# A hybrid decoder block on one core: the warm-up and the last tile of its first norm, one small load, and the product of a bias table

## The chip, the cores and the metric

The kernel runs on one core of a Trainium2 chip. The metric is the device time of one execution in microseconds, the median of several runs. A core has five engines that run in parallel and wait for each other by semaphores: TensorE (PE, matrix products and transposes; PEld is its weight load), VectorE (DVE), ScalarE (ACT), GpSimd (POOL) and SyncE (SP). DMAs are issued from the queues of SP, ACT and POOL. TensorE writes into PSUM, eight banks of 128 partitions by 512 floats, which VectorE and ScalarE empty.

## The reference

One layer on 512 tokens of width 1024, float32. Cut to what matters here:

```python
h = rmsnorm(x, attn_norm_g)                 # first norm
proj = h @ w_in                             # one combined projection, split into columns of
                                            # queries, 3 x (keys, values), gates, RWKV inputs, 2 merge gates
o_a = nsa_mixer(...)                        # compressed + selected + window attention, T5 bias table rel_bias
o_b = rwkv7_mixer(...)                      # RWKV-7 recurrence, 8 heads of 64
merged = sigmoid(gate_a) * (o_a @ w_proj_a) + sigmoid(gate_b) * (o_b @ w_proj_b)
x = x + merged @ w_out
h2 = rmsnorm(x, ffn_norm_g)
x = x + conv_ffn(h2, ...)                   # 2 x 2816 wide, causal conv of width 3, SiLU gate
```

In `nsa_mixer`, keys and values of overlapping blocks of 32 tokens go through `gelu(flat @ w1) @ w2` (the "compression"), and every score gets `rel_bias[t5_bucket(t - s)]` added.

## The kernel before

**Products.** The products with float32 weights are made from parts: a weight tile of 512 KB is loaded by SP into one of three `raw` buffers (`wload`, L267), split into a rounded half `hi` (`whi`, mostly ScalarE) and a remainder `lo` (`wlo`, L296, VectorE or GpSimd), and each product is the sum hi x hh + hi x hl + lo x hh, where `hh` and `hl` are the same two halves of the transposed activations. A `raw` buffer is loaded again when its split is done, a `whi` or `wlo` buffer (two each) is written again when TensorE is through with it. `weight_tiles` fixes the order of all weight tiles, and so the order of SP's queue.

**Order of the work.** Most of it is put in order by a planner that works with estimated costs; within `tc.manual_schedule(...)` the engines named there keep the order of the source. The DMAs of SP keep their place among the weight loads.

**First norm** (L326 to L376, in an order written by hand for TensorE, ScalarE, VectorE and GpSimd). `ident` (128x128) is loaded on ScalarE's queue (L154); 16 transposes of it by itself (`NWARM`, L329) run before any real work. For each of the four token tiles `t`: ScalarE sums squares (into `hs[t]`) and takes the square root, VectorE makes the reciprocal root (`rstd1`) and scales the tile (`ts`, L131; the last tile in two pieces of 512 columns), TensorE transposes it in blocks of 128 columns into eight banks `pts[k]` (`turn`, L335). For tiles 0 to 2 the transposes follow at once; those of the last tile come at the end, block by block. After tile 1, two more transposes turn the loaded parameter rows `pr0` (norm gain) and `pra` (RWKV parameters, eight small loads on GpSimd's queue, L162) into columns, in `pt`. ScalarE then splits the first weight tile (`hi`), and copies the gain to `ang`; VectorE copies the parameters to `prm` and makes `omm` = 1 - mu from them; GpSimd copies one element of `omm` into `lo` (L355), which its next instruction overwrites, and then makes `lo` in two halves (L357). For each block `k` ScalarE writes `hh[:, k]` and VectorE `hl[:, k]` (L136) from the bank. The first product `p0` takes the bank of block 0.

**Bias table** (L682 to L690, planned). A one-hot matrix (33 x 384) and the table (33 x 8, with a row for masked places) are loaded into corners of `QK`; one product (8 x 384) gives the bias by distance, ScalarE copies it to `vb`, and one DMA on ScalarE's queue writes it 16 times to a table `vd` in HBM. `bias_rows` reads that much later. The area of `vb` is written again by the key copies `kn` of `kv_proj(0, 256)`, which therefore wait for the DMA.

**Compression** (`compress`). Its four steps `s4` each take two weight tiles (`cmp_w1_k`, `cmp_w1_v`) and run as fillers between the steps of the RWKV recurrence. Within step `s4 == 1` SP is given the two loads of `cmp_w2` (64 KB each, L805) into `QK`; they are read after the last step. The recurrence's values `UV` are copied from PSUM by ScalarE and VectorE at each of its steps.

Of the kernel before, what the change touches and what calls it, by code (L numbers as in the profile page):

```python
# [11 lines left out]
F32 = mybir.dt.float32  # L12
# [9 lines left out]
D = 1024  # L22
NT = S // 128
# [18 lines left out]
ROWS = {}  # L42
# [39 lines left out]
def hybrid_block(ctx: ExitStack, tc: tile.TileContext, A: dict, out: bass.AP):  # L82
    nc = tc.nc
    v, sc, te = nc.vector, nc.scalar, nc.tensor
    NWARM = 16

    def dbg(name, ap):
        if name in DBG:
# [31 lines left out]
    def mm(o, l, r, start, stop):  # L120
        te.matmul(o, lhsT=l, rhs=r, start=start, stop=stop)  # L121

    def act(o, i, f=AF.Copy, **kw):
        sc.activation(o, i, f, **kw)  # L124
# [4 lines left out]
    def ts(o, a, s1, s2, op0=ALU.mult, op1=ALU.add):  # L129
        if s2 is None:  # L130
            v.tensor_scalar(o, a, s1, None, op0=op0)  # L131
        else:
            v.tensor_scalar(o, a, s1, s2, op0=op0, op1=op1)
# [6 lines left out]
    ident, mask, ones, cmask = kc[:, 0:128], kc[:, 128:256], kc[:, 256:384], kc[:, 384:416]  # L140
# [3 lines left out]
    xp_cm, xp = pool("x")  # L144
# [2 lines left out]
    v.memset(eps1, 1e-6)  # L147
    one = xp.tile([128, 1], F32, name="one")
    v.memset(one, 1.0)
    act(one, one, AF.Sqrt)  # L150
    pr0 = xp.tile([8, 128], F32, name="pr0")
    for t in range(NT):
# [4 lines left out]
    for name in ("rwkv_mu", "rwkv_w0", "rwkv_a0", "rwkv_k_k", "rwkv_k_a", "rwkv_r_k", "rwkv_ln_g", "rwkv_ln_b"):  # L157
        r0, n = ROWS[name]
# [10 lines left out]
    def cols(name):  # L169
        r0, n = ROWS[name]  # L170
        return prm[:, r0:r0 + n]
# [154 lines left out]
    with tc.manual_schedule(engines={getattr(mybir.EngineType, e) for e in ("PE", "Activation", "DVE", "Pool")}):  # L326
        pts = [mmb() if k < 4 else pa() if k < 6 else pb() for k in range(KT)]
        for i in range(NWARM):
            te.transpose(pts[7][:, 384:512], ident, ident)  # L329
        hi = wp.tile([128, KT, 128], F32R, name="whi", tag="whi", bufs=2)  # L330
        lo = wp.tile([128, KT, 128], F32R, name="wlo", tag="wlo", bufs=2)
        raw = loads.pop(0)[0]

        def turn(t, k):
            te.transpose(pts[k][:, 128 * t:128 * t + 128], hs[t][:, 128 * k:128 * k + 128], ident)  # L335

        for t in range(NT):
            r = ssx[:, t:t + 1]
            act(hs[t], xt[:, t], AF.Square, accum_out=r)
            rstd1(r)  # L340
            for c0 in ((0, 512) if t == NT - 1 else (0,)):
                c1 = 512 + c0 if t == NT - 1 else D
                ts(hs[t][:, c0:c1], xt[:, t, c0:c1], r, None)
            if t < NT - 1:
                for k in range(KT - t // 2):
                    turn(t, k)
            if t == 1:
                pt = pts[7][:, 384:512]
                te.transpose(pt[:, 0:8], pr0, ident[0:8, 0:8])
                te.transpose(pt[:, 8:8 + NR0], pra, ident[0:NR0, 0:NR0])  # L350
        act(hi, raw)
        act(ang, pt[:, 0:8])
        v.tensor_copy(prm[:, 0:NR0], pt[:, 8:8 + NR0])
        ts(omm, cols("rwkv_mu"), -1.0, 1.0)
        nc.gpsimd.tensor_copy(lo[:, 0, 0:1], omm[:, 0:1])  # L355
        for i in (slice(0, 4), slice(4, 8)):
            nc.gpsimd.tensor_tensor(lo[:, i], raw[:, i], hi[:, i].bitcast(F32), op=ALU.subtract)  # L357
        late.append(nc.gpsimd.tensor_copy)
        wsplit()
        for k in range(KT):  # L360
            for t in range(NT - 1 - k // 7, NT):
                turn(t, k)
            act(hh[:, k], pts[k], AF.Copy, scale=ang[:, k:k + 1])
            stt(hl[:, k], pts[k], ang[:, k:k + 1], hh[:, k].bitcast(F32), ALU.mult, ALU.subtract)
        ts(w0h, cols("rwkv_w0"), 0.5, None)
        ts(kah, cols("rwkv_k_a"), 0.5, None)
        ts(a0h, cols("rwkv_a0"), 0.5, None)
        ts(oma, cols("rwkv_k_a"), -0.5, 1.0)
        p0 = mmb()
        for k in range(KT):  # L370
            mm(p0, hi[:, k], hh[:, k], k == 0, False)
            if k:
                mm(p0, lo[:, k - 1], hh[:, k - 1], False, False)
            mm(p0, hi[:, k], hl[:, k], False, False)
        mm(p0, lo[:, KT - 1], hh[:, KT - 1], False, True)
# [237 lines left out]
    for k in range(31):  # L613
        m, n = 31 - k, k + 1
# [64 lines left out]
    windows(1, dense_fm(hh, hl))  # L679


    oh, rbx, vb = QK[0:33, 2048:2432], QK[0:33, 2440:2448], QK[0:8, 2560:2944]  # L682
    nc.gpsimd.memset(rbx[32:33], NEG)
    sc.dma_start(rbx[0:32], A["rel_bias"])
    sc.dma_start(oh, A["onehot"])
    pt = pa()
    mm(pt[0:8, 0:384], rbx, oh, True, True)
    act(vb, pt[0:8, 0:384])
    vd = dp.tile([8, 16 * 385], F32, name="vd")
    sc.dma_start(vd.rearrange("h (i m) -> h i m", m=385)[:, :, 0:384], vb[:, None, :].to_broadcast([8, 16, 384]))  # L690

    def kv_proj(b, n):
        bkv = yield from dense_tok_g(n, hh, hl)
# [85 lines left out]
    def compress():  # L779
        Rk = [sg1[:, 2 * a:2 * a + 2].rearrange("p m s -> p (m s)").rearrange("p (j g n) -> p j g n", j=16, g=2)  # L780
              for a in range(2)]
        for a, s_ in enumerate("kv"):
            v.memset(Rk[a][:, :, :, 31:32], 0.0)
            r0 = ROWS["cmp_pe_" + s_][0]
            for g in range(2):
                dv = Dc[:, a, g].rearrange("p (n j) -> p j n", j=8)
                for jh in range(2):
                    tt(Rk[a][:, 8 * jh:8 * jh + 8, g, 0:31], dv[:, :, jh:31 + jh],
                       prm[:, r0 + 8 * jh:r0 + 8 * jh + 8, None].to_broadcast([128, 8, 31]), ALU.add)
        cw2, hid, hidT, kcd = (QK[:, o:o + 256] for o in range(3072, 4096, 256))  # L790
        cw2 = cw2.rearrange("p (a m d) -> p a m d", a=2, m=2)
        hidT = hidT.rearrange("p (m a n) -> p m a n", m=2, a=2)
        kcd = kcd[0:32].rearrange("p (g a d) -> p g a d", g=2, a=2)
        kcs = cp.tile([32, 2], F32, name="kcs")
        yield
        hx = mmb()[:, 0:256]
        for s4 in range(4):
            w = [wnext(4, 256) for _ in range(2)]
            for j in range(4):
                for a in range(2):  # L800
                    mm(hx[64 * a:64 * a + 64], Rk[a][:, 4 * s4 + j].rearrange("p g n -> p (g n)"), w[a][:, j],
                       s4 + j == 0, s4 + j == 6)
            if s4 == 1:
                for a, s_ in enumerate("kv"):
                    nc.sync.dma_start(cw2[:, a], A["cmp_w2_" + s_][0].rearrange("(m p) d -> p m d", p=128))  # L805
            yield
        act(hid, hx, AF.Square)
        ts(hid, hid, 0.044715, 1.0)
        tt(hid, hid, hx, ALU.mult)
        act(hid, hid, AF.Tanh, scale=math.sqrt(2.0 / math.pi))  # L810
        stt(hid, hid, 1.0, hx, ALU.add, ALU.mult)
        yield
        pt = mmb()
        for m in range(2):
            te.transpose(pt[:, 128 * m:128 * m + 128], hid[:, 128 * m:128 * m + 128], ident)
        act(hidT.rearrange("p m a n -> p (m a n)"), pt[:, 0:256])
        yield
        kc_ps = mmb()
        for g in range(2):
            for m in range(2):  # L820
                mm(kc_ps[0:32, 64 * g:64 * g + 64], hidT[:, m, 0, 32 * g:32 * g + 32], cw2[:, 0, m], m == 0, m == 1)
        nc.gpsimd.memset(vcb, 0.0)
        for g in range(2):
            for e in range(2):
                bs = slice(64 * g + 32 * e, 64 * g + 32 * e + 32)
                for m in range(2):
                    mm(kc_ps[bs, 128:192], hidT[:, m, 1, 32 * g:32 * g + 32], cw2[:, 1, m], m == 0, m == 1)
        for g in range(2):
            for e in range(2):
                bs = slice(64 * g + 32 * e, 64 * g + 32 * e + 32)  # L830
                act(vcb[bs, 2 * g + e], kc_ps[bs, 128:192], AF.Copy, scale=0.5)
        for g in range(2):
            act(kcd[:, g, 0], kc_ps[0:32, 64 * g:64 * g + 64], AF.Copy, scale=0.5)
            act(kcd[:, g, 1], kcd[:, g, 0], AF.Square, accum_out=kcs[:, g:g + 1])
        rstd(kcs, DH)
        for g in range(2):
            ts(kcd[:, g, 1], kcd[:, g, 0], kcs[:, g:g + 1], None)
            ts(kcd[:, g, 0], kcd[:, g, 0], kcs[:, g:g + 1], None)
        yield
        pt = mmb()  # L840
        for g in range(2):
# [534 lines left out]
```

## Time and profile before

| | |
|---|---|
| median of 3 runs | 837.51 us (837.49 to 838.12) |
| profiled execution, its time | 838.0 us |
| its span in the profile | 836.2 us |
| TensorE busy | 822.0 us (98%) |
| VectorE busy | 515.8 us (62%) |
| ScalarE busy | 407.2 us (49%) |
| GpSimd busy | 51.5 us (6%) |

The profile is of one execution. Its span runs from the first to the last instruction; the device time holds some 1.8 us more around it. Busy time of an engine is the union of its instructions. A timeline row gives start, duration, engine, line, operation, written tile <- read tiles, shapes, the number of instructions merged into it, and in brackets the idle time before it and what ended that. Rows that end in q (SPq, ACTq) are DMA issues. Starts of consecutive products tell TensorE's pace; their durations overlap. The list of waits gives, for engine and line, what was waited for: microseconds in total, how many times, the longest.

### The profile page before, as it was taken

The page shows a single profiled execution, that of the slowest core. Times are in us where ns is not written, and L with a number is a line of the kernel's source. Part 1 is how long each engine was busy: PE and PEld are TensorE (multiplying, and loading weights), DVE is VectorE, ACT ScalarE, POOL GpSimd, SP SyncE. Part 2 cuts the span into 40 slices and gives each one's busy share as a digit, 9 for nine tenths or more (in the row PEclk, how much of TensorE's full clock was granted, in tenths as well). Part 3 has the DMA queues.
Part 4 walks back from the last instruction along what each step waited for, and adds up shares of the span by engine and source line. Part 5 has one row for each costly group of instructions (what it writes and reads, how often), then busy time and mean ns, then how long its engine had stood idle before and what let it go on. Part 6 is the DMA issues. An engine that isn't in the chain of part 4 may idle for free.

```text
span 836.2 us, 12860 instructions
## 1 busy us (share of the span) xinstructions
PE 822.0 (98%) x5091; PEld 668.2 (80%) x5091; DVE 515.8 (62%) x1003; ACT 407.2 (49%) x794; POOL 51.5 (6%) x68
## 2 busy tenths in 40 slices
PE   7999999999999999999999999999999999999998
PEld 6777778887778886777788988888888888888886
DVE  5477779974565878787665665566655566322222
ACT  6766654453455777676334454444444444221220
POOL 6200020140000100011000000000000000000000
PEclk9999999999999999999999999999999999999999
DMA  7432222346372310000275033333333332223421
GB/s 233 112 81 70 76 76 77 79 117 185 102 127 77 83 45 14 26 27 26 67 251 174 1 101 100 101 102 88 92 98 101 100 101 97 85 97 114 139 75 51
DMA packets 109264, 78.73 MB, mean 94 GB/s; under 512 B 3869, under 2 KB 97876, under 8 KB 109204
## 3 DMA queue, kind: packets, MB, share of 16 engines
q1 hardware_dynamic: 106800, 73.92, 30.6%
q10 hardware_dynamic: 1060, 2.55, 1.0%
q0 software_dynamic: 1344, 1.45, 0.8%
q8 instruction: 40, 0.66, 0.3%
q14 instruction: 20, 0.16, 0.1%
HBM read 74.56 MB, written 2.29 MB: 92 GB/s over the span
## 4 chain that ended last, share of the span: by engine, by line
PE 53%; DVE 0%; DVEq 0%; issue 0%
PE ps_mm L121 52%; PE ps_a L200 0%; PE ps_b L200 0%; PE ps_a L121 0%; PE ps_b L1180 0%; PE ps_mm L1180 0%; DVE x L127 0%; DVEq L1372 0%; PE ps_a L1132 0%
## 5 line engine op out<-in xcount | busy, mean ns | idle before, releaser
L121 PE MATMUL ps_mm<-hh,whi 128*128 128x512 f32 (+1 forms) x624 | 242.4, 391 | 1.4 <-DVE hl L136 0.8
L296 DVE TENSOR_TENSOR wlo<-raw,whi 128x1024 fp32r<-128x1024 f32 (+1 forms) x111 | 131.5, 1185 | 180.0 <-PE ps_mm L121 157.8
L121 PE MATMUL ps_mm<-hl,whi 128*128 128x512 f32 (+1 forms) x624 | 240.2, 387 | 0.0
L124 ACT ACTIVATE whi<-raw 128x1024 fp32r<-128x1024 f32 (+3 forms) x124 | 123.3, 996 | 155.9 <-PE ps_mm L121 142.1
L121 PE MATMUL ps_mm<-hh,wlo 128*128 128x512 f32 (+1 forms) x624 | 152.1, 384 | 0.0
L121 PEld LDWEIGHTS ps_mm<-hh,whi 128*128 128x128 f32 x624 | 117.2, 188 | 28.2 <-ACT whi L124 1.5
L121 PEld LDWEIGHTS ps_mm<-hl,whi 128*128 128x128 f32 x624 | 117.4, 188 | 23.0 <-issue 1.0
L121 PEld LDWEIGHTS ps_mm<-hh,wlo 128*128 128x128 f32 x624 | 115.1, 188 | 23.5
L121 PE MATMUL ps_mm<-whi,aT 128*128 128x512 f32 x352 | 84.5, 390 | 0.0
L121 PEld LDWEIGHTS ps_mm<-whi,aT 128*128 128x128 f32 x352 | 65.9, 188 | 14.3 <-issue 0.4
L136 DVE SCALAR_TENSOR_TENSOR cgv<-ps_mm,cw,cgv 128x511 f32<-128x511 f32 (+1 forms) x88 | 65.4, 746 | 1.6
L124 ACT ACTIVATE cgv<-ps_mm,cw 128x512 f32<-128x512 f32 x44 | 34.2, 780 | 23.3 <-PE ps_mm L121 23.3
L121 PE MATMUL ps_mm<-wlo,aT 128*128 128x512 f32 x176 | 44.3, 389 | 0.0
L124 ACT ACTIVATE P<-P,nm 128x512 f32<-128x512 f32 (+3 forms) x64 | 35.4, 553 | 15.0 <-DVE nm L1154 14.9
L124 ACT ACTIVATE aT<-cgv 128x512 fp32r<-128x512 f32 x22 | 13.9, 632 | 56.8 <-DVE cgv L127 56.8
L121 PEld LDWEIGHTS ps_mm<-wlo,aT 128*128 128x128 f32 x176 | 33.0, 188 | 6.9
L124 ACT ACTIVATE cgv<-cgv 128x512 f32<-128x512 f32 x22 | 13.9, 632 | 41.0 <-DVE cgv L136 41.0
L296 POOL TENSOR_TENSOR wlo<-raw,whi 128x512 fp32r<-128x512 f32 (+3 forms) x13 | 20.5, 1577 | 203.2 <-PE ps_mm L121 148.8
L1154 DVE CUSTOM_DVE_ANT_0 P<-ps_a,AB 128x512 f32<-128x512 f32 (+3 forms) x64 | 29.4, 484 | 4.2 <-PE ps_a L121 3.7
L127 DVE TENSOR_TENSOR x<-x,ps_mm 128x512 f32<-128x512 f32 (+1 forms) x17 | 11.1, 656 | 24.4 <-PE ps_mm L121 23.2
L127 DVE TENSOR_TENSOR aT<-cgv,aT 128x512 fp32r<-128x512 f32 x22 | 15.3, 693 | 14.7 <-ACT aT L124 14.7
L121 PE MATMUL ps_a<-KH,qst 128*128 128x512 f32 (+3 forms) x64 | 21.4, 349 | 1.6 <-DVE nm L1154 0.9
(354 smaller groups left out, 1202.1 us busy)
## 6 DMA issues: line engine op xcount, KB each, us to landing
raw<-in_w_up_dram SPq DMA_DIRECT2D x44, 512.0 KB, 3.8
raw<-in_w_in_dram SPq DMA_DIRECT2D x38, 512.0 KB, 4.1
raw<-in_w_down_dram SPq DMA_DIRECT2D x22, 512.0 KB, 3.6
raw<-in_w_out_dram SPq DMA_DIRECT2D x8, 512.0 KB, 4.1
xt<-in_x_dram SPq DMA_DIRECT2D x4, 512.0 KB, 5.3
raw<-in_cmp_w_v_dram SPq DMA_DIRECT2D x4, 512.0 KB, 3.9
raw<-in_w_proj_b_dram SPq DMA_DIRECT2D x8, 256.0 KB, 2.7
raw<-in_w_proj_a_dram SPq DMA_DIRECT2D x8, 256.0 KB, 2.7
```

Source lines behind the costliest of these rows:

```text
L121: te.matmul(o, lhsT=l, rhs=r, start=start, stop=stop)
L124: sc.activation(o, i, f, **kw)
L127: v.tensor_tensor(o, a, b, op=op)
L136: v.scalar_tensor_tensor(o, a, s, b, op0=op0, op1=op1)
L296: eng.tensor_tensor(lo, raw, hi.bitcast(F32), op=ALU.subtract)
L1154: v.tensor_tensor_reduce(out=P[:, i], in0=sp[:, N * (i - i0):N * (i - i0) + N], in1=BT[:, h, 384 - 128 * qt:512], scale=-1.0, scalar=-NEG, ...
```

## The change

- First norm: a tile `warm` (128 x 128, all ones) is filled by VectorE. The warm-up is 15 products of `warm` with itself in float32, in place of 16 transposes of `ident`.
- The last tile is scaled in pieces of 256 and 768 columns, not of 512 and 512.
- `ang` is copied before the split `hi`, not after it. `omm` is made from PSUM, not from `prm`. GpSimd's copy of one element of `omm` is gone.
- Bias table: two products of 8 x 192, the second on partitions 64 to 71, two copies and two DMAs.
- The two loads of `cmp_w2` are issued in step `s4 == 2`, not `s4 == 1`.

```diff
-    NWARM = 16
+    NWARM = 15
...
+    warm = xp.tile([128, 128], F32, name="warm")
+    v.memset(warm, 1.0)
     act(one, one, AF.Sqrt)
...
         for i in range(NWARM):
-            te.transpose(pts[7][:, 384:512], ident, ident)
+            mm(pts[7][:, 384:512], warm, warm, True, True)
...
-            for c0 in ((0, 512) if t == NT - 1 else (0,)):
-                c1 = 512 + c0 if t == NT - 1 else D
+            cut = (0, 256, D) if t == NT - 1 else (0, D)
+            for c0, c1 in zip(cut, cut[1:]):
                 ts(hs[t][:, c0:c1], xt[:, t, c0:c1], r, None)
...
+        act(ang, pt[:, 0:8])
         act(hi, raw)
-        act(ang, pt[:, 0:8])
         v.tensor_copy(prm[:, 0:NR0], pt[:, 8:8 + NR0])
-        ts(omm, cols("rwkv_mu"), -1.0, 1.0)
-        nc.gpsimd.tensor_copy(lo[:, 0, 0:1], omm[:, 0:1])
+        r0, n = ROWS["rwkv_mu"]
+        ts(omm, pt[:, 8 + r0:8 + r0 + n], -1.0, 1.0)
...
-    mm(pt[0:8, 0:384], rbx, oh, True, True)
-    act(vb, pt[0:8, 0:384])
     vd = dp.tile([8, 16 * 385], F32, name="vd")
-    sc.dma_start(vd.rearrange("h (i m) -> h i m", m=385)[:, :, 0:384], vb[:, None, :].to_broadcast([8, 16, 384]))
+    for i in range(2):
+        mm(pt[64 * i:64 * i + 8, 0:192], rbx, oh[:, 192 * i:192 * i + 192], True, True)
+    for i in range(2):
+        vb = QK[64 * i:64 * i + 8, 2560:2752]
+        act(vb, pt[64 * i:64 * i + 8, 0:192])
+        sc.dma_start(vd.rearrange("h (i m) -> h i m", m=385)[:, :, 192 * i:192 * i + 192],
+                     vb[:, None, :].to_broadcast([8, 16, 192]))
...
-            if s4 == 1:
+            if s4 == 2:
                 for a, s_ in enumerate("kv"):
                     nc.sync.dma_start(cw2[:, a], A["cmp_w2_" + s_][0].rearrange("(m p) d -> p m d", p=128))
```

Beside these edits the planner moves a few instructions: on ScalarE the key copy of the last token tile goes ahead of a weight split in the key projection, and the split of the merge-gate tile whose load follows `cmp_w1_v` of step 2 goes ahead of the copies `sg` and `UV` that stood before it; on VectorE that tile's `wlo` goes ahead of the copy of `UV`. In SP's queue the two `cmp_w2` loads come after the load of `AB` (the last `cmp_w1_k` tile), three loads later than before.

More of the change, by code (lines that the diff above doesn't have):

```diff
@@ L679, in hybrid_block @@
     windows(1, dense_fm(hh, hl))
-    oh, rbx, vb = QK[0:33, 2048:2432], QK[0:33, 2440:2448], QK[0:8, 2560:2944]
+    oh, rbx = QK[0:33, 2048:2432], QK[0:33, 2440:2448]
     nc.gpsimd.memset(rbx[32:33], NEG)
```

## The prediction

> **What bounds the kernel now.** I read the page first: the busy shares, then the chain that ended last.
>
> ```profile
> span 836.2 us, 12860 instructions
> ...
> PE 822.0 (98%) x5091; PEld 668.2 (80%) x5091; DVE 515.8 (62%) x1003; ACT 407.2 (49%) x794; POOL 51.5 (6%) x68
> ```
>
> ```profile
> 477.74 354.57 PE ps_mm L121 x1584
> ```
>
> TensorE is busy for 98% of the span, and the chain that ended last (second fence, its longest piece: start, length, what) is TensorE's too, product on product at 354.57/1584 = 0.224 us. So a microsecond counts only if TensorE idles in it, or spends it on something that can be had sooner. Next I listed whom TensorE waits for; these two of its waits touch the change.
>
> ```profile
> PE ps_b L329 <- DMA kc<-in_consts_dram: 4.8, 1, 4.8
> ...
> PE ps_mm L121 <- ACT whi L124: 0.7, 1, 0.7
> ```
>
> The first belongs to the first norm, the second is one stall at 200.84 us. The timeline of the first 15 us (start, duration, engine, line, operation) shows the norm.
>
> ```profile
> 0.84 0.06 DVE L149 MEMSET one<- 128x1 f32 x1
> 4.85 3.67 PE L329 MATMUL ps_b<-kc 128*128 128x128 f32 x16 [4.85 <-DMA kc<-in_consts_dram]
> 4.97 0.51 POOL L162 DMA_DIRECT2D pra<-in_rwkv_ln_b_dram  x1
> 6.80 0.75 DVE L131 TENSOR_SCALAR h<-xt,ssx 128x1024 f32<-128x1024 f32 x1
> 8.31 1.06 PE L335 MATMUL ps_mm<-kc,h 128*128 128x128 f32 x4
> 9.55 0.75 DVE L131 TENSOR_SCALAR h<-xt,ssx 128x1024 f32<-128x1024 f32 x1
> 10.03 0.29 ACT L124 ACTIVATE rx_y<-ssx,eps 128x1 f32<-128x1 f32 x1
> 10.43 1.06 ACT L124 ACTIVATE whi<-raw 128x1024 fp32r<-128x1024 f32 x1
> 10.87 0.42 PE L335 MATMUL ps_a<-kc,h 128*128 128x128 f32 x2
> 11.00 0.88 DVE L131 TENSOR_SCALAR h<-xt,ssx 128x512 f32<-128x512 f32 x2
> 11.89 0.18 ACT L124 ACTIVATE ang<-ps_b 128x8 f32<-128x8 f32 x1 [0.40 <-PE ps_b L350]
> 12.61 0.60 PE L335 MATMUL ps_mm<-kc,h 128*128 128x128 f32 x4
> 12.85 2.52 POOL L357 TENSOR_TENSOR wlo<-raw,whi 128x512 fp32r<-128x512 f32 x2
> 12.98 2.43 ACT L124 ACTIVATE hh<-ps_mm,ang 128x512 fp32r<-128x512 f32 x4 [0.91 <-PE ps_mm L335]
> 13.70 2.73 DVE L136 SCALAR_TENSOR_TENSOR hl<-ps_mm,ang,hh 128x512 fp32r<-128x512 f32 x4 [1.18 <-ACT hh L124]
> 14.50 0.50 PE L121 MATMUL ps_mm<-hh,whi 128*128 128x512 f32 x1 [0.75 <-DVE hl L136]
> ```
>
> The warm-up waits for the identity to land (4.85), runs to 8.31 and so holds up the first tile's transposes, although that tile was scaled at 7.55 (6.80 + 0.75). A transpose costs 0.22 us at first (16 from 4.85 to 8.31), and 0.11 in the row at 12.61, where four take 0.60, (0.60 - 0.27)/3 with 0.27 for the last one alone (a row of that sort stands below, at 221.10). The change falls into the pair at 10.87, so the clock doubled 6.0 us after TensorE's first work. Slow and late, TensorE is still on tiles 0 to 2 when the last tile is scaled (11.88), and reaches that tile only at 12.61. From there one chain leads to the first product: the first transpose (12.88), the copy hh (12.98), its remainder hl (13.70), which frees the bank, and the product at 14.50. From there to the stall at 200.84 the list holds no wait of TensorE over 0.3 us, so whatever moves 14.50 moves the end.
>
> **The change part by part: the start.** The warm tile is filled by VectorE right behind the row at 0.84, so TensorE can start near 1.1 instead of 4.85. The 15 products are true float32 products; the trace shows that form as two instructions that start 0.11 apart at full clock:
>
> ```profile
> 220.88 0.39 PE L121 MATMUL ps_b<-sg,g 128*128 128x128 f32 x2
> 221.10 0.27 PE L865 MATMUL ps_a<-kc,Ys 128*128 128x128 f32 x1
> ```
>
> That is 0.22 each, 0.43 at the slow clock, 6.4 us for 15: they end by 7.6 if all are slow, sooner if the clock doubles among them. If it again takes 6.0 us, it doubles at 7.1. Either way TensorE is free when tile 0 is ready at 7.55, and tiles 0 to 2 go through as they are scaled: tile 2 is scaled at 10.30, its seven transposes end near 11.2.
>
> Then the last tile's first piece decides. The rows for 1024 and twice 512 columns (0.75; 0.88 for two overlapping) give 0.35 for 256: scaled at 11.35, transposed by 11.74 (0.05 hand-over, 0.33 for a first transpose after a pause), hh at 11.82. The second piece ends at 11.89 as now.
>
> ScalarE must be free by then. "ang" now stands ahead of the 1.06 us copy "hi"; behind it in the queue are hi, hh and everything after. It needs the transposes of pr and pra, now done near 10.2, if pra has landed:
>
> ```profile
> pra<-in_rwkv_ln_b_dram POOLq DMA_DIRECT2D x1, 2.0 KB, 4.9
> ```
>
> 4.97 + 4.9 = 9.87, before that. So ang runs after the square root of the last tile (10.32), hi from 10.5 to 11.56, and hh is not held. Each microsecond that pra lands past 10.3 would cost one. VectorE has prm and omm done by 12.3, before hl needs it at 12.5. So the product comes at 14.50 - (12.98 - 11.82) = 13.34: **minus 1.16**. The bounds: nothing, if hi or hl hold it as much as the transposes did, and minus 1.5, if hand-overs are shorter.
>
> GpSimd's tiny cast, which waited for omm and kept lo back to 12.85, goes; lo starts when hi ends, 11.6, and its halves (1.26 each) are done at 12.9 and 14.1. Its first half is wanted by the fourth product, near 14.0: covered by 1.1 us.
>
> **The bias product.** One 8x384 product becomes two of 8x192 that write partitions 0 and 64, two ScalarE copies, two DMAs.
>
> ```profile
> 152.49 0.81 PE L121 MATMUL ps_a<-QK 33*8 33x384 f32 x2
> 153.23 0.39 PE L121 MATMUL ps_mm<-spare,hl 128*128 128x256 f32 x1
> ```
>
> ```profile
> 198.21 1.95 PE L121 MATMUL ps_mm<-raw,sg 128*64 128x256 f32 x16
> 200.84 0.50 PE L121 MATMUL ps_mm<-hh,whi 128*128 128x512 f32 x1 [0.68 <-ACT whi L124]
> ```
>
> It takes 0.74 of TensorE (152.49 to 153.23). In the row at 198.21 products write alternately the lower and upper 64 partitions, as the two halves will; 16 of 256 columns take 1.95, where one after the other at 0.21 they would take 3.4. The halves overlap likewise: 0.74 x 1.95/3.4 = 0.42, **minus 0.3**. Bounds: minus 0.37 (perfect overlap), plus 0.1 (no overlap, two more weight loads).
>
> ```profile
> 153.85 0.79 ACTq L690 DMA_DIRECT2D vd<-QK  x1
> 161.23 0.91 ACT L124 ACTIVATE whi<-raw 128x840 fp32r<-128x840 f32 x1 [2.35 <-DVE inv L136]
> 163.12 0.28 ACT L124 ACTIVATE QK<-ps_mm 128x128 f32<-128x128 f32 x1 [0.82 <-PE ps_mm L121]
> 166.78 0.91 ACT L124 ACTIVATE whi<-raw 128x840 fp32r<-128x840 f32 x1 [2.22 <-PE ps_mm L121]
> ```
>
> The second issue costs ScalarE 0.8 near 154.6, and the planner now puts the copy of 163.12 ahead of the split of 161.23, which comes 2 us later and pushes the rest of that queue by 1. I cost this at nothing: ScalarE then idles 2.22 until 166.78, and TensorE does not wait in this stretch. Without that pause it would be up to 2 us.
>
> **The small load.** Three issues of SP's queue, and the first reader of the small loads:
>
> ```profile
> 191.79 0.37 SPq L805 DMA_DIRECT2D QK<-in_cmp_w_k_dram  x1
> 192.78 0.40 SPq L267 DMA_DIRECT2D raw<-in_cmp_w_v_dram  x1
> 193.69 0.37 SPq L267 DMA_DIRECT2D raw<-in_w_in_dram  x1
> ```
>
> ```profile
> 234.17 0.92 PE L121 MATMUL ps_mm<-QK 128*32 128x64 f32 x24
> ```
>
> ```profile
> 199.73 1.06 ACT L124 ACTIVATE whi<-raw 128x1024 fp32r<-128x1024 f32 x1 [0.51 <-DMA raw<-in_w_in_dram]
> ```
>
> ```profile
> GB/s 0 0 109 0 0 55 0 0 0 0 0 0 0 0 75 150 123 55 89 55 68 287 389 382 403 362 393 370 333 299 249 278 280 147 27 68 246 321 328 362
> ```
>
> The load at 193.69 is the one the stall at 200.84 ends with: its split starts at 199.73, when it has landed. The two 64 KB loads (L805, the second issued right behind the first) go from ahead of it to behind the load issued next, of AB. The last row is the rate from 190 to 196 us in slices of 0.15: the small loads pass at about 280 GB/s, 128 KB/280 = 0.47 us, and behind them the rate falls to 147, 27 and 68 because the next load came late, about 0.3 us lost. So the load lands some 0.6 earlier: **minus 0.6** of the stall's 0.68. Bounds: 0, if its own start is held by something else, and minus 0.68. The moved loads are read only by the products at 234.17, nearly 40 us later, and what stands behind them in SP's queue waits for TensorE to free a buffer anyway. On ScalarE the planner now puts this split ahead of the copies that stood before it (sg, UV), which slip by 2; TensorE reads UV after the first 13 products of that weight tile, 2.9 us past their start near 200.2, and VectorE has it by about 201.9: covered by 1.2.
>
> **The sum** is made against the profiled execution, 838.0 (836.2 span and 1.8 around it): 838.0 - 1.16 - 0.3 - 0.6 = **835.9**. The runs shown have a median of 837.51 (837.49 to 838.12), so the profiled one is at their upper end. I do not lower the forecast for that: a likely reason is a late doubling of the clock, which delays the transposes before the change and not after it. Against 837.51 it is 0.19% less.
>
> **Rivals.** *A rival that ends slower: the clock falls back.* With an early warm-up TensorE pauses between tiles (about 0.4 us of each 1.38) from 7.6 to 13.3. If too little work there halves the clock, products cost 0.45 instead of 0.224 until it doubles again; after one 6.0 us spell like the one above, 3.0 are lost, and the transposes of tiles 2 and 3 cost 0.6 to 0.9 more: 835.9 + 3.8 = 839.7. It decides from a loss of 3.3 up. For it: 6.0 us of unbroken work went by before the clock doubled, so a little work may not be enough to hold it. Against: each pause is short, and a pause of 0.75 before 14.50 did no harm. The Trainium skill, "TensorE: Matmul & The Clock Gate", Part 1, says that the rate halves only after an idle window of about 3.4 us, which speaks against this rival; no run here shows a fall-back.
>
> *GpSimd gets in VectorE's way.* Without the cast, lo may start while VectorE still scales the last tile. If hi ended before 11.27, where the 768-column piece starts, that piece would wait for a lo half, 1.26, and hh for the third block, due at 12.96, would come at about 13.6: 835.9 + 0.7 = 836.6. Against: hi now follows ang and ends at 11.56. The Trainium skill, "SBUF — State Buffer", says that the two engines share a port pair which one instruction holds to its end; by that rule lo instead waits to 11.9, which its 1.1 us of cover absorbs.
>
> *The loads are hidden anyway*: the load at 193.69 does not land sooner and the halves do not overlap. Only the start is left: 836.8.
>
> *The start changes little*, because ang waits for pra, or hi and hl bind: 838.0 - 0.2 - 0.9 = 836.9 to 837.1.
>
> **How the numbers follow.** Forecast 60%, own range 835.3 to 836.5; a larger gain (every bound at its best, 1.5 + 0.37 + 0.68: 835.5) 8%; loads hidden 14%; start changes little, or the port, 9% together; clock falls back 9%. A measurement tells 0.2% from no change, 1.68 us, 835.83 on the runs shown; a new set of runs of before could centre up to 838.1, which moves that line to 836.4. So of the forecast's 60 I count 47 as faster and 13 as same: faster 0.47 + 0.08 = 0.55, same 0.13 + 0.14 + 0.09 = 0.36, slower 0.09. The range 834.9 to 837.5 takes in all but the fall-back, with the spread of the three runs shown (0.63) below the largest gain and half of it above the smallest.
>
> **What would show it.** Right: first product near 13.3, transposes of tile 2 at 0.11 each, no TensorE wait over 0.2 where 200.84 was, four bias instructions in about 0.4. Wrong: a warm-up that ends past 8, ang later than 10.7, products 0.45 apart after 13, a stall of 0.5 or more on that split, or a new wait for UV or for the copies near 165.

## The result and the profile after

Times in us, medians, with the number of runs:

| kernel | median | lowest to highest | runs |
|---|---|---|---|
| before | 837.6 | 836.85 to 838.48 | 22 |
| after | 836.4 | 836.18 to 836.55 | 22 |

The ratio is 0.9985 (95% interval 0.9978 to 0.9991): 1.2 us less, 0.15%. There is a second gain, in the third column: the runs of after lie within 0.37 of each other, those of before within 1.63. The profiled execution of after took 836.53, that of before 838.0.

First the head of the page of after.

```profile
span 834.7 us, 12900 instructions
```

The timeline of after's first 15 us (start, duration, engine, line, operation):

```profile
1.12 6.35 PE L121 MATMUL ps_b<-warm 128*128 128x128 f32 x30 [1.12 <-DVE warm L151]
4.88 1.06 ACT L124 ACTIVATE h<-xt 128x1024 f32<-128x1024 f32 x1 [2.18 <-DMA xt<-in_x_dram]
9.17 1.06 ACT L124 ACTIVATE h<-xt 128x1024 f32<-128x1024 f32 x1
10.58 0.66 PE L337 MATMUL ps_mm<-kc,h 128*128 128x128 f32 x4
10.69 0.18 ACT L124 ACTIVATE ang<-ps_b 128x8 f32<-128x8 f32 x1
10.76 1.05 ACT L124 ACTIVATE whi<-raw 128x1024 fp32r<-128x1024 f32 x1
11.33 0.88 DVE L131 TENSOR_SCALAR h<-xt,ssx 128x256 f32<-128x256 f32 x2
11.83 0.88 PE L337 MATMUL ps_mm<-kc,h 128*128 128x128 f32 x4 [0.26 <-ACT whi L124]
11.90 2.69 POOL L359 TENSOR_TENSOR wlo<-raw,whi 128x512 fp32r<-128x512 f32 x2 [6.15 <-ACT whi L124]
12.22 2.42 ACT L124 ACTIVATE hh<-ps_mm,ang 128x512 fp32r<-128x512 f32 x4 [0.41 <-PE ps_mm L337]
13.76 0.50 PE L121 MATMUL ps_mm<-hh,whi 128*128 128x512 f32 x1 [0.51 <-DVE hl L136]
```

The first product comes at 13.76, 0.74 before the 14.50 of before. Further on in the same timeline, TensorE at the bias product, at the compression's products of the first group of weights, and where the stall of 0.68 was:

```profile
151.77 0.49 PE L121 MATMUL ps_a<-QK 33*8 33x192 f32 x4
152.19 0.39 PE L121 MATMUL ps_mm<-spare,hl 128*128 128x256 f32 x1
...
179.97 0.65 PE L121 MATMUL ps_mm<-raw,sg 128*64 128x256 f32 x2
180.81 1.94 PE L121 MATMUL ps_mm<-raw,sg 128*64 128x256 f32 x14 [0.19 <-DVE sg L127]
182.68 0.39 PE L121 MATMUL ps_mm<-whi,hh 128*128 128x280 f32 x1
...
197.52 1.95 PE L121 MATMUL ps_mm<-raw,sg 128*64 128x256 f32 x16
199.55 0.50 PE L121 MATMUL ps_mm<-hh,whi 128*128 128x512 f32 x1
```

Read against the rows of before that the prediction quotes, the lead of after is 0.74 at the first product, 1.04 behind the bias product (153.23 to 152.19), 0.69 at the second group of compression products (198.21 to 197.52), 1.29 behind the stall (200.84 to 199.55), 1.5 at the end of the span. So 0.35 was lost again between 153 and 198, and the row at 180.81 shows where: the products of the first group wait there for sums `sg` that VectorE delivers. From their start to the first product of the next weights it is 2.71 (179.97 to 182.68). TensorE in before at the same place:

```profile
181.01 2.38 PE L121 MATMUL ps_mm<-raw,sg 128*64 128x256 f32 x16
183.32 0.40 PE L121 MATMUL ps_mm<-whi,hh 128*128 128x280 f32 x1
```

It is 2.31 there (181.01 to 183.32), where 16 such products that nothing holds take 1.88 (180.09 to 181.97, in the second fence on two Newton steps below). Three questions follow: whether the start is worth 0.74 in every execution, whether the bias product is worth anything, and why the load is worth what it is.

### The profile page after: what moved, and what is told of

Same layout as the page of the kernel before. It is cut to its first block, busy times and chain, and to the rows that moved or that the text cites. A ratio compares the mean times of both kernels' runs of the same rounds, so it can differ in the third digit from the quotient of the medians.

```text
span 834.7 us, 12900 instructions
## 1 busy us (share of the span) xinstructions
PE 824.0 (99%) x5107; PEld 669.6 (80%) x5107; DVE 515.7 (62%) x1004; ACT 406.7 (49%) x795; POOL 51.4 (6%) x67
## 4 chain that ended last, share of the span: by engine, by line
PE 53%; DVE 0%; DVEq 0%; issue 0%
PE ps_mm L121 52%; PE ps_a L202 0%; PE ps_b L202 0%; PE ps_a L121 0%; PE ps_b L1186 0%; PE ps_mm L1186 0%; DVE x L127 0%; DVEq L1378 0%; PE ps_a L1138 0%
## 5 line engine op out<-in xcount | busy, mean ns | idle before, releaser
L124 ACT ACTIVATE QK<-ps_mm 128x64 f32<-128x64 f32 (+5 forms) x56 | 14.9, 310 | 18.3 <-PE ps_mm L121 18.2
```

## The experiments

Three sets, each with its own runs of before on the same chip. "Less" is the median against that before; the interval is that of the ratio. An interval that holds 1.0000 does not tell the kernel from before.

| kernel | median | before beside it | less | lowest to highest | ratio, 95% interval |
|---|---|---|---|---|---|
| start alone | 837.35 | 837.70 | 0.35 | 837.01 to 837.88 | 0.9994, 0.9985 to 1.0003 |
| small load alone | 836.58 | 837.70 | 1.12 | 836.38 to 837.18 | 0.9984, 0.9975 to 0.9993 |
| bias halves alone | 837.55 | 837.70 | 0.15 | 836.94 to 837.99 | 0.9996, 0.9988 to 1.0005 |
| warm-up alone | 837.37 | 837.70 | 0.33 | 837.05 to 837.97 | 0.9993, 0.9984 to 1.0002 |
| after | 836.35 | 837.62 | 1.27 | 836.17 to 836.90 | 0.9985, 0.9976 to 0.9994 |
| after, old start | 836.62 | 837.62 | 1.00 | 836.23 to 837.65 | 0.9988, 0.9979 to 0.9997 |
| after, bias in one piece | 836.43 | 837.62 | 1.19 | 836.17 to 836.70 | 0.9985, 0.9976 to 0.9994 |
| after, two Newton steps | 835.76 | 837.62 | 1.86 | 835.54 to 836.02 | 0.9977, 0.9969 to 0.9986 |
| the same, bias in one piece | 835.82 | 837.75 | 1.93 | 835.64 to 835.96 | 0.9977, 0.9968 to 0.9986 |
| before, small loads from ScalarE | 840.45 | 837.75 | -2.70 | 839.93 to 841.89 | 1.0035, 1.0022 to 1.0047 |
| after, no warm-up | 837.72 | 837.75 | 0.03 | 837.21 to 838.53 | 1.0000, 0.9991 to 1.0009 |
| after, 8 warm-up products | 837.82 | 837.75 | -0.07 | 836.80 to 838.07 | 0.9999, 0.9990 to 1.0007 |

Each has 10 or 11 runs, the one with the loads from ScalarE 5; the befores 26 or 33. The first three, each alone, add up to 1.62, and the whole change gives 1.27; with intervals this wide that is no contradiction.

And what each profiled execution shows at the two places in question, from the timeline and the trace's granted clock: how long after TensorE's first work the clock doubled, ScalarE's first square (it waits for x tile 0), the first product, and how long behind the start of the second group of compression products the next product came (1.88 where nothing holds it).

| kernel | clock doubled after | first square | first product | product minus square | next product behind |
|---|---|---|---|---|---|
| before | 6.10 | 4.65 | 14.50 | 9.86 | 2.62 |
| start alone | 3.59 | 4.80 | 13.62 | 8.82 | 3.37 |
| small load alone | 3.64 | 4.87 | 13.70 | 8.83 | 1.88 |
| bias halves alone | 3.59 | 4.67 | 13.53 | 8.86 | 2.77 |
| warm-up alone | 6.08 | 4.81 | 13.70 | 8.89 | 2.45 |
| after, first profile | 5.77 | 4.88 | 13.76 | 8.88 | 2.03 |
| after, second profile | 3.67 | 5.03 | 13.74 | 8.70 | 1.88 |
| after, old start | 4.18 | 4.75 | 13.73 | 8.98 | 1.97 |
| after, bias in one piece | 4.90 | 4.94 | 13.64 | 8.70 | 1.88 |
| after, two Newton steps | 3.16 | 4.87 | 13.66 | 8.79 | 1.97 |
| the same, bias in one piece | 4.07 | 4.89 | 13.59 | 8.70 | 1.88 |
| before, small loads from ScalarE | 5.32 | 4.62 | 14.09 | 9.47 | 1.88 |

### Start alone, warm-up alone, and the old start in after

Start alone is before with all of the start's edits and nothing else; warm-up alone has only this:

```
-            te.transpose(pts[7][:, 384:512], ident, ident)
+            mm(pts[7][:, 384:512], warm, warm, True, True)
```

with the filled tile and 15 repetitions; "after, old start" is after without the start's edits.

> The kernel before with the whole start and nothing else: warm-up of 15 float32 products on the filled tile, ang ahead of hi, omm from the bank, no cast on GpSimd, last tile cut at 256. The trace of after has the first product at 13.76 against 14.50. Theory A (the start is worth what the trace of after shows and all of it reaches the end): 0.74 less than before, first product near 13.8, and the 22 or so runs lie within about 0.5 us of each other, since TensorE no longer waits for the identity and a late clock. Theory B (the prediction's size was right and the x tiles merely landed late in the one profile of after): 1.1 to 1.2 less, first product near 13.3 to 13.5 with the first square of ScalarE at 4.65. Theory C (the gain at the start is lost again where VectorE sets the pace, near 180): under 0.4 less.

> The kernel before with only the warm-up replaced (15 float32 products on a filled tile instead of 16 transposes of the identity); ang, omm, the cast and the cut at 512 as before. Theory A (the backlog of slow transposes was what held the first product, and what replaces it is the chain of the last tile): last tile's first transposes near 11.7 to 11.9, first product near 13.8 to 14.0, 0.5 to 0.7 less than before; runs within about 0.5 us of each other. Rival (the order of ang and hi and the cut carry the gain): under 0.3 less, first product after 14.2.

> The kernel after with the start of before (16 transposes of the identity, ang behind hi, cast on GpSimd, cut at 512). Theory A (the old start loses only where the clock doubles late: product minus first square is 9.85 in before, where it doubled 6.1 after TensorE's first work, but 8.83 and 8.86 where it doubled 3.6 after): slower than after by 0.2 to 0.5 in the median, with runs scattered over 0.8 us or more above the fastest of after. Rival (the prediction's term: the old start costs 1.16, or the 0.74 of the two traces, in every run): 0.7 or more slower, runs as close together as those of after.

Measured: 0.35 and 0.33 less than before, and the old start costs after 0.27, as its theory A had it. Each of the three lies at the edge of what these runs resolve (the intervals of the first two hold 1.0000); that all three come out near 0.3 is the evidence. For the start alone the size is the one expected if the gain were lost near 180, but the place is another, as the next section shows; the warm-up alone came out between its theory and its rival. The first product came at 13.62 with the whole start and at 13.70 with the warm-up alone; the order of `ang`, the cut and the cast carry nothing that can be seen. What the start is worth depends on when the clock doubles, as the fifth column shows: with the old start the first product stands 8.83 to 8.98 behind the first square where the clock doubled within 4.2 of TensorE's first work (three kernels), 9.47 where it took 5.32, and 9.86 in before, where it took 6.10. With the new start it stands 8.70 to 8.89 behind, whether that took 3.16 or 6.08. The old start in the kernel with the small load alone shows why: its warm-up begins as late as in before, and yet its transposes of tile 0 are fast.

```profile
4.87 1.06 ACT L124 ACTIVATE h<-xt 128x1024 f32<-128x1024 f32 x1 [2.17 <-DMA xt<-in_x_dram]
5.07 3.68 PE L329 MATMUL ps_b<-kc 128*128 128x128 f32 x16 [5.07 <-DMA kc<-in_consts_dram]
8.53 0.69 PE L335 MATMUL ps_mm<-kc,h 128*128 128x128 f32 x4
```

Four transposes take 0.69 here (1.06 in before), TensorE keeps pace with the tiles, and the first product, at 13.70, is where after has it. So the start removes a loss of 0 to 1.0 that changes from execution to execution. The scatter fits, but is no proof: 0.37 and 0.73 in the two sets of after, 1.42 with the old start in after, yet only 0.80 in the small load alone, which has the old start too.

### Small load alone

```
-            if s4 == 1:
+            if s4 == 2:
```

> The kernel before with the two small loads of the compression issued one step later and nothing else. Theory A (the load of w_in landed late because of them): the TensorE wait of 0.68 on the ACT split near 200.84 is gone and the time is 0.6 less; the runs scatter as widely as those of before (over 1 us), since the start is as it was. Rival (the split was late for another reason, and in the kernel after it moved with the reordered ScalarE queue or the earlier start): under 0.2 less, the wait stays at 0.5 or more.

1.12 less, nearly twice what was expected, and the stall is gone (next product 1.88 behind). The runs lie within 0.80, where over 1 was expected, and closer than the 1.49 of the before beside it, so the stall made scatter too. Its size in one profile is not its size in the next. Here is TensorE at the second group of products in the start alone, which like the warm-up alone and the bias halves alone has the small loads at their old place:

```profile
197.47 2.43 PE L121 MATMUL ps_mm<-raw,sg 128*64 128x256 f32 x16
200.83 0.50 PE L121 MATMUL ps_mm<-hh,whi 128*128 128x512 f32 x1 [0.94 <-ACT whi L124]
```

By the table's last column the start alone, the warm-up alone and the bias halves alone lose 1.49, 0.57 and 0.89 beyond the 1.88, and before 0.74: 0.92 on average. The start alone loses 0.48 of it on the products themselves (2.43 instead of 1.95), whose weights come late too, and with it all that the start had won: the lead over before is 0.74 at 197.47 and 0.01 at 200.83. The kernels of the table with the load moved lose 0 to 0.15 (one outside it, without warm-up, lost 1.16; see below).

SP's queue shows how the load comes sooner; first before (only the row that the prediction lacks), then after.

```profile
191.12 0.37 SPq L267 DMA_DIRECT2D raw<-in_cmp_w_k_dram  x1
```

```profile
190.47 0.37 SPq L269 DMA_DIRECT2D raw<-in_cmp_w_k_dram  x1
190.94 0.45 SPq L269 DMA_DIRECT2D raw<-in_cmp_w_v_dram  x1
191.49 0.45 SPq L269 DMA_DIRECT2D raw<-in_w_in_dram  x1
```

The load of `w_in` is issued 1.02 behind the `k` weights in after and was issued 2.57 behind them in before (193.69): two more issues and two pauses stood between. Against the products at 198.21 and 197.52 it is issued 1.5 sooner. ScalarE's split of it then starts when it has landed; in after:

```profile
198.44 1.06 ACT L124 ACTIVATE whi<-raw 128x1024 fp32r<-128x1024 f32 x1 [7.62 <-DMA raw<-in_w_in_dram]
```

From the issue of the `k` weights to this split it is 7.97 here (190.47 to 198.44) and 7.43 to 7.95 in the six other profiles of the table with the small loads moved; the four with the old place have 8.39 to 9.34, before 8.61 (191.12 to 199.73). From its own issue to the split the load takes 6.41 to 6.95 in those seven (6.70 on average) and 5.84 to 6.80 in the four (6.20), so it does not land sooner after its issue without the small loads ahead of it: the whole gain stands in the earlier issue, and 0.5 of that goes back. Whether it would land later still if it were issued as early with their bytes ahead, no run shows. These times scatter by 0.5 and more from profile to profile, and with them the stall.

The planner's new order on ScalarE is no rival for this: in all four profiles with the old place ScalarE stood idle before the split, 0.33 to 1.25, until the load had landed.

### The small loads from ScalarE's queue

Before, with the loads left where they were in the program, but on another queue:

```
-                    nc.sync.dma_start(cw2[:, a], A["cmp_w2_" + s_][0].rearrange("(m p) d -> p m d", p=128))
+                    sc.dma_start(cw2[:, a], A["cmp_w2_" + s_][0].rearrange("(m p) d -> p m d", p=128))
```

> The kernel before with the two small loads of the compression issued at the same point of the program, but from ScalarE's queue instead of SP's. Theory I (what delays the load of w_in is SP's queue: the two issues and the gaps about them put its issue 2.6 after that of the k weights, 1.0 in after): SP issues w_in about 1.0 after the k weights, the v weights land 1.6 to 2.1 behind the k weights instead of 2.8, and the time is 0.8 to 1.1 less than before. Theory II (it is their bytes: 128 KB in packets of 256 B ahead of it): at most 0.4 less, the v weights land 2.4 or more behind the k weights.

2.7 more, which neither theory had, and the time does not tell the two apart: the planner put the issues so early into ScalarE's queue that the queue waited with them. ScalarE, TensorE and SP of this kernel, in order of time:

```profile
179.30 0.39 ACTq L805 DMA_DIRECT2D QK<-in_cmp_w_k_dram  x1
180.26 0.76 ACT L124 ACTIVATE AB<-ps_a 32x256 f32<-32x256 f32 x2 [5.31 <-DVE sg L783]
183.23 2.90 PE L121 MATMUL ps_mm<-raw,sg 128*64 128x256 f32 x16 [2.61 <-ACT gts L124]
194.55 0.37 SPq L267 DMA_DIRECT2D raw<-in_cmp_w_k_dram  x1
195.56 0.46 SPq L267 DMA_DIRECT2D raw<-in_w_in_dram  x1
```

ScalarE stood idle for 5.31 with the issue and what follows it, by the profile until VectorE was done with `sg`; TensorE lost 2.61 by it and then ran slow until 187.6 (below). With SP's queue free, `w_in` went out 1.01 behind the `k` weights, its split started 7.36 behind them (201.91), and no stall is left. But the small loads' bytes had passed long before, so this kernel cannot part the late issue from the bytes. That the two together cost the stall is shown; how they share it stays open, though the times from issue to split in the section above speak for the late issue.

### The bias product

"Bias halves alone" is before with the two halves; "after, bias in one piece" is after without them.

> The kernel before with the bias table product in two halves and nothing else. Theory A (what TensorE saves reaches the end): 0.3 less. Theory B (VectorE's unbroken chain from the inverse through the keys' norms sets the products of the gate at 181.0; TensorE comes 0.3 earlier and waits there): the four bias instructions still take about 0.42 instead of 0.74, the second pair of products raw,sg waits for sg by about 0.3, and the time is within 0.15 of before. The runs scatter as those of before.

> The kernel after with the bias table product in one piece as before. Theory B (VectorE sets the pair of products raw,sg near 180.8, so what TensorE saves at the bias is waited away there): within 0.1 of after, and the wait for sg of 0.2 to 0.4 that after has is gone. Rival A (the 0.32 that the four instructions save reaches the end): 0.3 slower than after.

0.15 less, and after loses 0.08 without the halves: nothing that the runs can tell from no change. In the bias halves alone the four instructions take 0.42 (the next product starts 0.42 behind them) and the wait for `sg` is there, as expected if VectorE sets the pace. TensorE in after with the bias in one piece:

```profile
180.14 2.50 PE L121 MATMUL ps_mm<-raw,sg 128*64 128x256 f32 x16
182.57 0.39 PE L121 MATMUL ps_mm<-whi,hh 128*128 128x280 f32 x1
```

From 180.14 to 182.57 it is 2.43. So against 1.88 TensorE loses 0.55 here without the halves and 0.83 with them (2.71): 0.28 of the 0.32 that they save is waited away.

### VectorE relieved: two Newton steps

```
-        rstd(kss[:, b].rearrange("p t h -> p (t h)"), DH)
+        rstd(kss[:, b].rearrange("p t h -> p (t h)"), DH, steps=2 + b)
...
-        rstd(qss.rearrange("p t h -> p (t h)"), DH)
+        rstd(qss.rearrange("p t h -> p (t h)"), DH, steps=2)
```

A Newton step refines the inverse root; the third step of these two norms is left out, six small VectorE instructions that stand ahead of the sums. The kernel then computes these roots less exactly: it is a probe, not a proposal.

> The kernel after, unchanged, as the yardstick for the three beside it: about 1.2 to 1.3 less than before, runs within 0.4 us of each other. Its profile also shows again how long after TensorE's first work the clock doubles and where the x tiles land; if the first product stands a fixed 8.8 to 8.9 after ScalarE's first square whatever the clock does (8.88 in after, 8.82 and 8.89 in the two kernels with the warm-up alone or with the whole start), the start no longer depends on the clock.

> The kernel after with two Newton steps instead of three in the inverse root of the first keys' and the queries' norms (the third step of these two is left out): six VectorE instructions less, 0.55 to 0.7 us, in the chain that ends with the sums sg near 180.8. Theory B: TensorE's wait for sg goes, the products raw,sg start 0.3 to 0.4 sooner after the end of the O_KW products, and the time is 0.25 to 0.4 less than after. Rival C (it is given back behind it: the split of w_in ends at 199.50 in after and TensorE is ready for it at 199.55, so an earlier TensorE waits for the load): a TensorE wait for the ACT split near 199 of 0.2 or more and less than 0.15 gained. Rival A (VectorE is not what it waits for): no change, the second pair still starts 0.57 behind the second product.

> The kernel of two Newton steps (the third step of the first keys' and the queries' norms left out) with the bias table product in one piece. Theory B (the halves save their 0.32 on TensorE, but VectorE hides it in after): with VectorE out of the way the halves count, so this kernel is 0.2 to 0.35 slower than the one of two steps with halves, whose median was 835.76 beside a before of 837.62; that is 1.5 to 1.7 less than before. Rival (the halves are worth nothing anywhere): as fast as that one, 1.85 less than before.

After itself, again: 1.27 less, as expected, with runs within 0.73 where 0.4 was expected. With two steps it is 0.59 less than after in the same set, more than the 0.25 to 0.4 expected, and the lowest time of all: VectorE held TensorE by more than the one wait of 0.2 that the list shows. The rows account for it: the first group loses 0.13 (2.01) instead of 0.83, and 0.09 goes back at 198.75, the split of `w_in`, which leaves 0.6. Here is TensorE with two steps, then the same with the bias in one piece:

```profile
179.87 2.08 PE L121 MATMUL ps_mm<-raw,sg 128*64 128x256 f32 x16
181.88 0.40 PE L121 MATMUL ps_mm<-whi,hh 128*128 128x280 f32 x1
...
198.75 0.50 PE L121 MATMUL ps_mm<-hh,whi 128*128 128x512 f32 x1
```

```profile
180.09 1.95 PE L121 MATMUL ps_mm<-raw,sg 128*64 128x256 f32 x16
181.97 0.40 PE L121 MATMUL ps_mm<-whi,hh 128*128 128x280 f32 x1
...
198.75 0.50 PE L121 MATMUL ps_mm<-hh,whi 128*128 128x512 f32 x1
```

The expectation that the halves would count now fell: 1.93 against 1.86 less. In this pair the kernel with the halves leads by 0.22 behind the bias product (152.09 against 152.31), by 0.09 at 181.9, since VectorE still holds it a little, and by nothing at 198.75, where the split of `w_in` sets the time. The wait for the load stands close behind the one for VectorE.

Where VectorE is held up itself shows in after, in the timeline of VectorE and GpSimd:

```profile
174.63 1.39 POOL L298 TENSOR_TENSOR wlo<-raw,whi 128x560 fp32r<-128x560 f32 x1 [5.00 <-ACT AB L124]
174.70 1.35 DVE L133 TENSOR_SCALAR rs_m<-kss 128x8 f32<-128x8 f32 x1
175.97 0.17 DVE L133 TENSOR_SCALAR rs_m<-qss 128x32 f32<-128x32 f32 x1
```

An operation on 128x8 takes 1.35, although the one behind it on four times as many columns takes 0.17: it ends with GpSimd's subtraction beside it (174.63 + 1.39 = 176.02, 174.70 + 1.35 = 176.05). The Trainium skill, "SBUF — State Buffer", section "Who interferes with whom", says that these two engines share one pair of ports and that one instruction holds it to its end; these rows agree, at a price of 1.2 in the chain that TensorE waits for. Before pays it too, on another small operation (175.80 to 177.13, beside a subtraction that ends at 177.10), so it did not come with the change. Whether that subtraction elsewhere would free TensorE no run here shows.

### Less warm-up

```
-    NWARM = 15
+    NWARM = 0
```

The other kernel has `NWARM = 8`.

> The kernel after without any warm-up product. TensorE's first work is then the transposes of tile 0 near 7.8. Theory A (the clock doubles 3.2 to 6.1 after the first work, short pauses or not): doubled between 11.0 and 13.9, tiles 0 to 2 go through at 0.22 a transpose, the first product comes 0.3 to 1.2 later than in after, and the time is 0.4 to 1.5 more with a scatter of about 1 us. Rival (pauses keep the clock down until the unbroken products): doubled 3.2 to 6.1 after the first product, near 18 to 20, and 2 to 3.5 more than after.

> The kernel after with 8 warm-up products instead of 15: they end near 4.5, and TensorE then idles for about 3.3 until tile 0. Theory A (the clock doubles 3.2 to 6.1 after the first work and a pause of that length neither stops nor undoes it): as after, within 0.15. Rival (the clock falls back, or does not rise, after a pause of 3.3): transposes of tile 0 at 0.22, clock doubled 3.2 to 6.1 behind them, 0.4 to 1.5 more than after, with a scatter of about 1 us.

Both lose all that the change had won, 1.2 to 1.3: without a warm-up as theory A had it, with 8 products as the rival had it. The clock does not need the warm-up as such (without it the clock doubled 3.67 after tile 0's first transpose), but half of one is worth no more than none. The timeline of TensorE with 8 products:

```profile
1.12 3.78 PE L121 MATMUL ps_b<-warm 128*128 128x128 f32 x16 [1.12 <-DVE warm L151]
7.72 1.12 PE L337 MATMUL ps_mm<-kc,h 128*128 128x128 f32 x4 [2.82 <-DVE rx_m L133]
15.38 0.50 PE L121 MATMUL ps_mm<-hh,whi 128*128 128x512 f32 x1 [0.66 <-DVE hl L136]
```

All 16 instructions of the warm-up ran slow (3.78 / 16 = 0.24), a pause of 2.82 followed, and nothing was left of it: the transposes at 7.72 still take 0.22 each ((1.12 - 0.45)/3), the clock doubled only at 13.80, and the first product came at 15.38. Without any warm-up it came at 14.48, and that profile also waited 1.09 for the split of `w_in`, the moved load notwithstanding:

```profile
198.25 1.95 PE L121 MATMUL ps_mm<-raw,sg 128*64 128x256 f32 x16
201.29 0.50 PE L121 MATMUL ps_mm<-hh,whi 128*128 128x512 f32 x1 [1.09 <-ACT whi L124]
```

The load landed late there: the split started 9.02 behind the issue of the `k` weights. A late start alone does not make this stall, since the kernel with 8 products comes to the same place later still (199.07) and has none; what made it stays open. So moving the loads does not rule the stall out.

## Why the prediction was right, and where its terms were not

The time (835.9 forecast, 836.4 measured) lay in the range and the gain was real but small. The forecast is 0.5 too low, and its parts erred more than its sum. That is in part luck: against the medians it counted 0.8 too much on the start and 0.2 on the bias, and it started from an execution 0.4 above the median, while it counted 0.5 too little on the load.

**The start, forecast 1.16 less.** The trace gave 0.74. The steps held: warm-up from 1.12 to 7.5, tile 2's transposes at 0.11 ((0.66 - 0.33)/3), `ang` at 10.69, `hi` done at 11.81 and no longer ahead of a waiting `hh`. What is missing is 0.42. Of it, 0.33 is a last tile scaled at 11.33 rather than 11.00: x tile 0 landed 0.23 later, and the square of the last tile slipped 0.10 more (9.17 against 8.84). The first square came at 4.62 to 4.87 in the five profiles with the old start and at 4.75 to 5.03 in the nine that fill `warm`, 0.16 later on average, so the landing of one execution accounts for some of it, and whether the new start itself delays the tiles a little stays open. The rest lies with the first piece: its transposes start 0.50 behind its scaling (11.33 to 11.83), where 0.40 was counted. As a gain over the median of before the term is further off: the step that failed is the one that took the late clock of one execution, which cost it 1.0, for the state of before, and did not ask what other executions pay. Against medians the start is worth 0.3. The prediction's reading of why before scatters, a late clock that delays the transposes before the change and not after it, fits the profiles: product minus square is 8.83 to 8.98 with an early clock, 9.47 and 9.86 with a late one. The stall's scatter, which came on top, it did not see.

**The bias product, forecast 0.3 less.** The four instructions take 0.42 as worked out, and the gain is lost at 180.81. The step that failed took a list that holds no TensorE wait over 0.3 for the absence of waits, and from it drew "whatever moves 14.50 moves the end". For the start that nearly held as far as 198, since VectorE's work moved along with TensorE's: the start alone leads before by 0.88 at its first product (13.62) and by 0.74 at 197.47. It did not hold for what TensorE alone saves. In before VectorE already held these products up by 0.43 (2.31 instead of 1.88), in waits between single products that stay below what the list shows, so there was no slack for a TensorE that comes sooner.

**The small load, forecast 0.6 less.** In the pair of traces it gave 0.60 (1.29 - 0.69); in the medians 1.12. That the small loads delay this one was right; the term was mis-sized. It was bounded by the stall of one execution, 0.68, and four executions with the old place lost 0.57 to 1.49. Bytes and pause were counted as 0.6, while the issue itself came 1.5 sooner, and from there the load took no less time to land.

**The edits costed at nothing.** The planner's new order near 161 to 166 was hidden (the lead stays 1.04 through it, 181.01 against 179.97), and TensorE's list of waits in after has none for `UV` or `lo`.

**The rivals.** *Clock falls back*: not in after, though TensorE paused there for parts of each tile; but it exists: after an idle time of 2.61 the clock fell in the kernel with the loads from ScalarE. *GpSimd in the way*: not at the start, where `lo` began at 11.90 and VectorE's pieces took the 0.88 of before, but the same two engines do hold each other up at 174.7. *Loads hidden anyway* was the reverse of what happened; that its time of 836.8 is near is chance.

## What to carry to other kernels

A term that hangs on the moment a clock rises or a transfer lands should be priced over several executions, and against the median, not against the one that was profiled. Before counting a saving on the busiest engine, find the next place where it meets another engine and see by how much that one was early; here VectorE was late already, and a load stood 0.6 behind it. A small transfer that nobody waits for still has its place in the queue, and what stands behind it is issued later for it: 1.5 here.

## What the runs showed of the hardware

The clock doubled 3.16 to 6.10 after TensorE's first work where that work was unbroken, at a moment that changed from one execution to the next. In the kernel with the small loads on ScalarE it also fell back in the middle of the run. Here are some windows of it (each row: the stretch, its length, the busy time of TensorE, of its weight loads, of VectorE, ScalarE and GpSimd); the granted clock stands in the third column from the right:

```profile
184.00:185.00 1.00, 1.00 (x9) 0.90 (x7) 0.00 (x0) 0.40 (x3) 1.00 (x2) 0.61 0.06 16
185.00:186.00 1.00, 1.00 (x6) 0.30 (x2) 0.00 (x0) 0.00 (x0) 0.28 (x1) 0.50 0.00 0
187.00:188.00 1.00, 1.00 (x7) 1.00 (x7) 0.00 (x0) 0.00 (x0) 0.00 (x0) 0.69 0.59 65
```

TensorE had worked for 180 us; after an idle time of 2.61 it ran at half the clock from 184.2 to 187.6, for 3.4. The Trainium skill, "TensorE: Matmul & The Clock Gate", Part 1, tells of a free-running window of 3413 ns whose activity sets the clock. The length of this spell and the range of 3.2 to 6.1 agree with that, and so does the trace's clock record: the spell lasted 3.41 (184.22 to 187.63), and the full clock before it 174.08 (10.14 to 184.22), 51 times 3.413, so the changes stand on a grid that runs on by itself. That the rate falls only after an idle window does not quite agree: of the 3.41 that ended at 184.22 TensorE was busy for 0.99, and the clock fell. It was busy for 1.87 of the 3.41 from 4.79 to 8.20 in the second profile of after, and the clock stayed. Nor does the clock need a whole busy stretch to rise: 3.16 of 3.41 were enough (0.87 to 4.28, two Newton steps), 2.67 were not (6.97 to 10.39, 8 warm-up products). The 8 products themselves fill 2.44 and 1.34 of the two stretches on this grid that they lie in, and so could not raise it.

A shorter pause, of 1.33 before tile 0 in the start alone, did no harm: the transposes behind it are fast.

```profile
7.77 0.66 PE L337 MATMUL ps_mm<-kc,h 128*128 128x128 f32 x4 [1.33 <-DVE rx_m L133]
```
